# Twenty feed-forward tiles as seven block products instead of eight, with activations and residual parked in memory

## The chip, the core and the metric

The kernel runs on one core of one Trainium2 chip. The number that counts is the device time of one execution in microseconds (us), the median of several runs. The profile is one execution taken by the hardware profiler; it records every instruction of the engines: TensorE (PE) for matmuls with its weight loads (PEld), VectorE (DVE), ScalarE (ACT), GpSimd (POOL), and the queue of SyncE (SP) that issues the DMA transfers.

## The reference

One encoder block on 512 tokens of width 2048, in float32. What matters here is its second half, the gated feed-forward (`D_FF` is 5632):

```python
x = x + jnp.concatenate([y_f, y_g], axis=-1) @ w_out[l]
h2 = rmsnorm(x, norm_ffn[l])
x = x + (jax.nn.silu(h2 @ w_gate[l]) * (h2 @ w_up[l])) @ w_down[l]
return rmsnorm(x, norm_final)
```

## The kernel before

Every product of two float32 matrices is done as three matmuls. Each operand is split into `hi`, a rounded copy (ACT writes it), and `lo`, the remainder `raw - hi` (DVE writes it); `hi*hi`, `hi*lo` and `lo*hi` accumulate in one PSUM bank (`mm3`). So a weight tile of 128x1024 costs one ACT copy and one DVE subtraction before TensorE may use it (`split`, `split_weights`). The buffers for `hi` and for `lo` are three deep.

The feed-forward has 44 tiles of 128 features. `GateUp(f, up, kk)` is one unit: half of the depth (8 of 16 slices of 128) of the gate or the up projection of tile `f`, 24 matmuls of 128x512. The second half of a tile's gate is followed by a DVE multiply with the token scales `rg` and a tanh on ACT; the second half of its up by two DVE operations that complete the activation in `act`. Two tiles share one slot of 128x2x512, four tiles make a quad.

The down projection already uses block products. For each of ten quads and each half `np_` of the output columns there are seven instead of eight (`Product`, in the order 1, 2, 5, 6, 3, 7, 4), 12 matmuls of 128x512 each. Before a product runs, DVE forms a sum of activation blocks (`x`) for four of the seven and a sum of weight blocks (`r[..]`) for four of the seven; ACT and DVE split both. After it, DVE adds the two PSUM banks into the residual `x2`, or into `usum`, which `Fold` later adds to three of the four blocks. Product 2 goes on accumulating in the banks of product 1, and product 3 in those of product 5, after DVE has read what stood there. The last two pairs of tiles are multiplied in the usual way (`Split`, `Last`, `Tail`).

The program order is written by hand. `drive` walks through `items`; ahead of each item `k` it emits the preparation of item `k + 2` on ACT and DVE, then the item's matmuls (`run`), then what follows them (`out`), and what follows on the next item's turn (`late`). Each engine works through its own list in this order. In `items` a quad's 14 products stand one by one between the 16 `GateUp` units of the next quad, so a product always has a unit on both sides. Raw weights come through the SP queue, at most three `GateUp` tiles ahead (`load_unit`), and the blocks of `w_down` up to eight items ahead.

The residual `x2` (8 slots of 4 KB per partition) and the activations stay in SBUF throughout. The pool of such slots (`spool`) holds 25.

Of the kernel before, what the change touches and what calls it, by code (L numbers as in the profile page):

```python
# [16 lines left out]
P = 128  # L17
# [16 lines left out]

QUADS = 10


@with_exitstack
def encoder_block(ctx, tc, a, out):
# [129 lines left out]
    def split(src, dst):  # L169
        nc.scalar.copy(dst[0], src)  # L170
        nc.vector.tensor_sub(dst[1], src, dst[0])  # L171
# [49 lines left out]
    def both(x, c):  # L221
        return x[0][:, c], x[1][:, c]
# [210 lines left out]
    def x2c(m, n):  # L433
        return x2[m][n // 2][:, (n % 2) * S : (n % 2 + 1) * S]

    xss = const.tile([P, NT, 4], F32, name="xss")
    h2 = []

    def transposes(n):
        for i in range(4):  # L440
            c = 4 * n + i
            ps = bank(f"xt{c}")
            for m in range(NT):
                nc.tensor.transpose(ps[:, m * P : (m + 1) * P], x2c(m, n)[:, i * P : (i + 1) * P], ident)
# [31 lines left out]


    fss = const.tile([P, NT, 4], F32, name="fss")
    act = [None] * FT

# [23 lines left out]

    pgu = {}
    acts = {}

    class GateUp(RawUnit):
        def __init__(self, f, up, kk):
# [12 lines left out]
        def out(self):  # L522
            if self.kk == 0:
                return
            f = self.f
            if not self.up:
                if f == 0:
                    ffn_scales()
                if f % 2 == 0:
                    acts[f // 2] = slot(f"act{f // 2}", F32, (P, 2, S))  # L530
                self.z = acts[f // 2][:, f % 2, :]
                self.s = small.tile([P, S], F32, tag="act", bufs=1, name=f"s{f}")
                nc.vector.tensor_mul(self.z, pgu[0], rg)
                nc.scalar.activation(self.s, self.z, AF.Tanh, scale=0.5)
                pgu["gate"] = self
            else:
                s, z = pgu["gate"].s, pgu["gate"].z
                nc.vector.scalar_tensor_tensor(s, pgu[1], 0.5, rg, op0=ALU.mult, op1=ALU.mult)
                nc.vector.tensor_mul(z, z, s)

        def late(self):
            if self.kk and not self.up:
                nc.vector.scalar_tensor_tensor(self.z, self.s, 1.0, self.z, op0=ALU.add, op1=ALU.mult)
# [8 lines left out]


    ORDER = (1, 2, 5, 6, 3, 7, 4)
    usum = [slot(f"u{np_}", F32, (P, 2, S)) for np_ in range(2)]
    for np_ in range(2):
        nc.gpsimd.memset(usum[np_], 0.0)

    def out_block(k, t, np_):

        return x2c(2 * (k // 10 - 1) + t, 2 * np_ + k % 10 - 1)

    PRODUCTS = {}

    class Product(Item):
# [89 lines left out]
    def down(i, m, n, w):  # L655
        ps = bank(f"l{i}_{m}_{n}")
        for j in range(2):
            c = slice(j * S, (j + 1) * S)
            mm3(ps, both(rest[2 * i + j], slice(m * P, (m + 1) * P)), (w.hi[:, c], w.lo[:, c]), j == 0, j == 1)
        return ps  # L660

    class Last(RawUnit):
# [9 lines left out]
        def out(self):  # L672
            tails[self.n].prep()
            for m in range(NT):
                nc.vector.tensor_add(x2c(m, self.n), self.ps[m], x2c(m, self.n))

    class Tail(RawUnit):

# [19 lines left out]
                rest.append(p)  # L698


    items = []
    pending = []
    for q in range(FT // 4):
        for i in range(16):
            items.append(GateUp(4 * q + i // 4, i // 2 % 2, i % 2))
            if i > 0 and pending:
                items.append(pending.pop(0))
            if q == QUADS and i in (8, 14):
                items.append(Split(0) if i == 8 else Fold(0))
        pending = [Product(q, np_, i) for np_ in range(2) for i in ORDER]  # L710
    items += [Fold(1), Split(1)]
    items += [Last(n) for n in range(4)]

    tails = [Tail(n) for n in range(4)]
    units = [x for x in items if isinstance(x, RawUnit)]
    units[-1:] = [tails[0], units[-1], *tails[1:]]

    def load_unit():
        if units:
            units.pop(0).load()  # L720

    def drive(items, lead=8):

        for _ in range(3):
            load_unit()
        works = [x for x in items if not isinstance(x, (Split, Fold))]
        loaded = set()
        for x in works[:2]:
            yield x
            load_unit()  # L730
        behind = []
        k = 0
        for x in items:
            if x in works:
                if k + 2 < len(works):
                    y = works[k + 2]
                    y.prep()
                    if isinstance(y, RawUnit):
                        load_unit()
                for y in works[k : k + lead]:  # L740
                    if isinstance(y, Product) and y not in loaded:
                        y.load()
                        loaded.add(y)
                k += 1
            for y in behind:
                y.late()
            x.run()
            x.out()
            behind = [x]

    ENG = mybir.EngineType
    with tc.manual_schedule(engines={ENG.SP, ENG.PE, ENG.DVE, ENG.Activation, ENG.Pool}):
        for x in drive(items):
            x.prep()


    gB = [slot(f"gB{i}") for i in range(2)]
# [95 lines left out]
```

## Time and profile before

| | |
|---|---|
| runs | 1886.45 us median of 3 (1886.31 to 1886.63) |
| profiled execution | 1886.81 us, span of the instructions 1885.0 us |
| TensorE busy | 1864.7 us, 8370 matmuls |
| VectorE busy | 1210.0 us, 1541 instructions |
| ScalarE busy | 657.0 us, 844 instructions |
| moved by DMA | 197.52 MB, mean 105 GB/s |
| granted TensorE clock | 0.997 of full speed |

The profiled execution is 0.36 us above the median of the runs. The feed-forward begins at 486.3 us of the span and runs to its end. A matmul's row in the profile shows its latency; matmuls overlap, so the pace of TensorE is read from the distance between the starts of two neighbours, or from a count in a stretch that is fully busy.

### The profile page before, as it was taken

The page shows a single profiled execution, that of the slowest core. Times are in us where ns is not written, and L with a number is a line of the kernel's source. Part 1 is how long each engine was busy: PE and PEld are TensorE (multiplying, and loading weights), DVE is VectorE, ACT ScalarE, POOL GpSimd, SP SyncE. Part 2 cuts the span into 40 slices and gives each one's busy share as a digit, 9 for nine tenths or more (in the row PEclk, how much of TensorE's full clock was granted, in tenths as well). Part 3 has the DMA queues.
Part 4 walks back from the last instruction along what each step waited for, and adds up shares of the span by engine and source line. Part 5 has one row for each costly group of instructions (what it writes and reads, how often), then busy time and mean ns, then how long its engine had stood idle before and what let it go on. Part 6 is the DMA issues. An engine that isn't in the chain of part 4 may idle for free.

```text
span 1885.0 us, 20877 instructions
## 1 busy us (share of the span) xinstructions
PE 1864.7 (99%) x8370; PEld 1546.7 (82%) x8370; DVE 1210.0 (64%) x1541; ACT 657.0 (35%) x844; POOL 68.6 (4%) x54
## 2 busy tenths in 40 slices
PE   9999999999999999999999999999999999999996
PEld 7888788888888888888888888888888888888885
DVE  7455654333435767767767677677676776776787
ACT  6335633232323333333333333333332332332334
POOL 5001101000000000000000000000000000000004
PEclk9999999999999999999999999999999999999998
DMA  6222224422232232233133222332333223222323
GB/s 246 91 79 101 90 72 141 145 90 90 91 121 90 101 112 91 91 121 112 67 112 112 101 100 90 112 112 72 107 112 111 90 90 118 106 86 97 108 89 124
DMA packets 55969, 197.52 MB, mean 105 GB/s; under 512 B 6592, under 2 KB 6720, under 8 KB 55872
## 3 DMA queue, kind: packets, MB, share of 16 engines
q1 hardware_dynamic: 55584, 195.15, 29.7%
q8 instruction: 65, 1.06, 0.2%
q0 software_dynamic: 288, 1.05, 0.2%
q14 instruction: 32, 0.26, 0.0%
HBM read 191.98 MB, written 4.19 MB: 104 GB/s over the span
## 4 chain that ended last, share of the span: by engine, by line
PE 97%; DVE 1%; ACT 1%; DMA 0%; issue 0%; SPq 0%; POOL 0%; ACTq 0%; DVEq 0%
PE up L82 8%; PE g L82 8%; PE up L83 8%; PE g L83 8%; PE g L84 8%; PE up L84 8%; PE d L625 7%; PE d L624 7%; PE d L623 7%; PE o L84 3%; PE o L82 3%; PE o L83 3%; PE v L82 2%; PE v L84 2%; PE v L83 2%; PE a L84 1%
## 5 line engine op out<-in xcount | busy, mean ns | idle before, releaser
L82 PE MATMUL up<-h2hi,hi_up 128*128 128x512 f32 x704 | 274.0, 389 | 0.0
L82 PE MATMUL g<-h2hi,hi_g 128*128 128x512 f32 x704 | 274.0, 389 | 0.0
L84 PE MATMUL g<-h2hi,lo_g 128*128 128x512 f32 x704 | 273.9, 389 | 0.0
L84 PE MATMUL up<-h2hi,lo_up 128*128 128x512 f32 x704 | 273.9, 389 | 0.0
L83 PE MATMUL up<-h2lo,hi_up 128*128 128x512 f32 x704 | 273.9, 389 | 0.0
L83 PE MATMUL g<-h2lo,hi_g 128*128 128x512 f32 x704 | 273.9, 389 | 0.0
L171 DVE TENSOR_TENSOR lo_d<-w,hi_d 128x1024 fp32r<-128x1024 f32 x140 | 171.5, 1225 | 82.9 <-ACT hi_d L170 82.9
L623 PE MATMUL d<-hi_d,X 128*128 128x512 f32 x560 | 217.8, 389 | 0.0
L624 PE MATMUL d<-lo_d,X 128*128 128x512 f32 x560 | 217.8, 389 | 0.0
L625 PE MATMUL d<-hi_d,X 128*128 128x512 f32 x560 | 217.8, 389 | 0.0
L170 ACT CAST hi_d<-w 128x1024 fp32r<-128x1024 f32 x140 | 147.2, 1051 | 184.9 <-issue 40.0
L84 PEld LDWEIGHTS up<-h2hi,lo_up 128*128 128x128 f32 x704 | 132.1, 188 | 27.5
L84 PEld LDWEIGHTS g<-h2hi,lo_g 128*128 128x128 f32 x704 | 132.1, 188 | 27.5
L82 PEld LDWEIGHTS up<-h2hi,hi_up 128*128 128x128 f32 x704 | 132.1, 188 | 27.4
L82 PEld LDWEIGHTS g<-h2hi,hi_g 128*128 128x128 f32 x704 | 132.1, 188 | 27.4
L83 PEld LDWEIGHTS g<-h2lo,hi_g 128*128 128x128 f32 x704 | 132.1, 188 | 27.4
L83 PEld LDWEIGHTS up<-h2lo,hi_up 128*128 128x128 f32 x704 | 132.1, 188 | 27.4
L170 ACT CAST X<-x 128x512 fp32r<-128x512 f32 x80 | 49.8, 622 | 270.4 <-DVE x L587 102.7
L171 DVE TENSOR_TENSOR lo_up<-raw_up,hi_up 128x1024 fp32r<-128x1024 f32 x88 | 107.3, 1220 | 47.6 <-ACT hi_up L170 47.6
L170 ACT CAST hi_g<-raw_g 128x1024 fp32r<-128x1024 f32 x88 | 92.5, 1052 | 112.7 <-PE d L625 56.5
L634 DVE TENSOR_TENSOR x<-d,x 128x512 f32<-128x512 f32 x200 | 130.8, 684 | 0.0
L170 ACT CAST hi_up<-raw_up 128x1024 fp32r<-128x1024 f32 x88 | 92.5, 1052 | 104.9 <-PE g L83 57.7
(254 smaller groups left out, 2930.7 us busy)
## 6 DMA issues: line engine op xcount, KB each, us to landing
raw_g<-in_w_gate SPq DMA_DIRECT2D x88, 512.0 KB, 3.3
raw_up<-in_w_up SPq DMA_DIRECT2D x88, 512.0 KB, 3.3
w<-in_w_down SPq DMA_DIRECT2D x80, 512.0 KB, 4.5
raw_o<-in_w_out SPq DMA_DIRECT2D x32, 512.0 KB, 3.2
raw_v<-in_w_v SPq DMA_DIRECT2D x16, 512.0 KB, 3.2
raw_u<-in_w_u SPq DMA_DIRECT2D x16, 512.0 KB, 3.3
raw_a<-in_w_a SPq DMA_DIRECT2D x15, 512.0 KB, 3.8
x<-in_x SPq DMA_DIRECT2D x8, 512.0 KB, 8.2
```

The costliest lines, as they stand in the source:

```text
L82: mm(ps, lhs[0], rhs[0], start=first, stop=False)
L83: mm(ps, lhs[0], rhs[1], start=False, stop=False)
L84: mm(ps, lhs[1], rhs[0], start=False, stop=last)
L170: nc.scalar.copy(dst[0], src)
L171: nc.vector.tensor_sub(dst[1], src, dst[0])
L623: mm(p, X[:, 0, j, l], hi, start=j == 0 and not more, stop=False, skip_group_check=True)
L624: mm(p, X[:, 0, j, l], lo, start=False, stop=False, skip_group_check=True)
L625: mm(p, X[:, 1, j, l], hi, start=False, stop=j == 1, skip_group_check=True)
L634: nc.vector.tensor_add(d, self.ps[t], d)
```

## The change

The gate and the up projection of tiles 4 to 23 become block products too. A pair of tiles (256 features), 2048 deep, times 512 tokens is cut in two along each of the three sides: 8 products of 128 features x 1024 deep x 256 tokens, of which 7 are done (`Block`, in the order 1, 6, 2, 7, 5, 4, 3). A block is 24 matmuls of 128x256. One `Matrix` is the gate or the up of one pair; there are 20.

- The sums of token blocks (`Forms`, 8 of them) are made once, while the first four tiles run as before. Their split copies and raw sums lie in 16 of the 26 slots until the last block has run.
- The sums of weight blocks are made by DVE for every matrix: two adds ahead of block 6, one ahead of block 7 (its result is used by block 4), one subtraction ahead of block 5.
- After a block DVE (after blocks 1 and 2 ACT) takes 128x256 out of PSUM. After block 3 come the scales and the tanh, now on 128x1024.
- No product of the down projection stands among the blocks. All 140 stand among the 80 units of tiles 24 to 43: of the 76 gaps between units that get any, 64 get two products and 12 get one.
- To make room, the residual goes to DRAM (`xd`, 8 stores) before the feed-forward and comes back in 16 loads of 256 KB when tile 24 has begun (`Outputs`); activations of the ten quads go to DRAM as they are made (`ad`, 20 stores of 512 KB, from the POOL queue) and come back two at a time with the first product of a quad (20 loads).
- `Fold(0)` moves from between the last units to the end, beside `Fold(1)`.

The names: `lo_gb7_6` is the remainder of the weights for block 6 of the gate of pair 7 (`gb`), `upb` is the up; `o_gb7` collects the gate, `t_` holds partial sums, `th` the tanh; `d3_0_1` is product 1 of quad 3, column half 0, `X` its activation operand, `ac` a reloaded activation pair.

First place: VectorE, where the gate of a pair ends and the up begins. Before, the gate of tile 14 ended like this (a product of quad 2 in between):

```order
L171 TENSOR_TENSOR lo_up14_0_6390<-raw_up14_0_6221,hi_up14_0_6389 128x1024
L533 TENSOR_TENSOR act7_6419<-g14_6341,rstdB_99 128x512
L585 TENSOR_TENSOR x2_1_5_6423<-act4_5097,act5_5553 128x512
L596 TENSOR_TENSOR w11_2_1_6164<-w11_2_1_6164,w12_2_1_6282 128x1024
L171 TENSOR_TENSOR X2_1_5_6425<-x2_1_5_6423,X2_1_5_6425 128x512
L171 TENSOR_TENSOR lo_d2_1_5_6430<-w11_2_1_6164,hi_d2_1_5_6429 128x1024
L543 SCALAR_TENSOR_TENSOR act7_6419<-s14_6420,act7_6419 128x512
```

Now the gate of tiles 14 and 15 ends like this:

```order
L633 TENSOR_TENSOR w12_upb7_6512<-w12_upb7_6512,w22_upb7_6514 128x1024
L634 TENSOR_TENSOR w11_upb7_6510<-w11_upb7_6510,w12_upb7_6512 128x1024
L174 TENSOR_TENSOR lo_upb7_6_6732<-w11_upb7_6510,hi_upb7_6_6731 128x1024
L671 TENSOR_TENSOR o_gb7_6550<-gb7_5_6673,t_gb7_6551 128x256
L676 TENSOR_TENSOR o_gb7_6550<-o_gb7_6550,rstdB_101 128x1024
L174 TENSOR_TENSOR lo_upb7_2_6770<-w21_upb7_6548,hi_upb7_2_6769 128x1024
L687 SCALAR_TENSOR_TENSOR o_gb7_6550<-th7_6766,o_gb7_6550 128x1024
L636 TENSOR_TENSOR w21_upb7_6548<-w21_upb7_6548,w11_upb7_6510 128x1024
L174 TENSOR_TENSOR lo_upb7_7_6806<-w12_upb7_6512,hi_upb7_7_6805 128x1024
L661 TENSOR_TENSOR t_upb7_6777<-upb7_6_6809,t_upb7_6777 128x256
L638 TENSOR_TENSOR w11_upb7_6510<-w11_upb7_6510,w22_upb7_6514 128x1024
L174 TENSOR_TENSOR lo_upb7_5_6837<-w11_upb7_6510,hi_upb7_5_6836 128x1024
```

The work that ends the gate (L671, L676, L687) now stands between the sums and remainders of the weights for the up's blocks 6, 2, 7 and 5, each of which TensorE takes up within a block or two.

Second place: VectorE, where products 1 and 2 of quad 3 are prepared. Before, a unit's remainder and its activation stand between them:

```order
L171 TENSOR_TENSOR X3_0_1_6765<-act6_5963,X3_0_1_6765 128x512
L171 TENSOR_TENSOR lo_d3_0_1_6769<-w11_3_0_6620,hi_d3_0_1_6768 128x1024
L171 TENSOR_TENSOR lo_up16_0_6798<-raw_up16_0_6680,hi_up16_0_6797 128x1024
L533 TENSOR_TENSOR act8_6829<-g16_6772,rstdB_99 128x512
L171 TENSOR_TENSOR X3_0_2_6833<-act7_6419,X3_0_2_6833 128x512
L171 TENSOR_TENSOR lo_d3_0_2_6837<-w21_3_0_6682,hi_d3_0_2_6836 128x1024
L543 SCALAR_TENSOR_TENSOR act8_6829<-s16_6830,act8_6829 128x512
L634 TENSOR_TENSOR u0_3607<-d3_0_1_0_6841,u0_3607 128x512
L634 TENSOR_TENSOR u0_3607<-d3_0_1_1_6842,u0_3607 128x512
```

Now the two products are neighbours:

```order
L174 TENSOR_TENSOR X3_0_1_10717<-ac6_10550,X3_0_1_10717 128x512
L174 TENSOR_TENSOR lo_d3_0_1_10721<-w11_3_0_10554,hi_d3_0_1_10720 128x1024
L782 TENSOR_TENSOR x21_1_8859<-d2_1_4_0_10724,x21_1_8859 128x512
L782 TENSOR_TENSOR x21_1_8859<-d2_1_4_1_10725,x21_1_8859 128x512
L174 TENSOR_TENSOR X3_0_2_10740<-ac7_10552,X3_0_2_10740 128x512
L174 TENSOR_TENSOR lo_d3_0_2_10744<-w21_3_0_10580,hi_d3_0_2_10743 128x1024
L174 TENSOR_TENSOR lo_up30_1_10775<-raw_up30_1_10611,hi_up30_1_10774 128x1024
L782 TENSOR_TENSOR u0_8834<-d3_0_1_0_10778,u0_8834 128x512
L782 TENSOR_TENSOR u0_8834<-d3_0_1_1_10779,u0_8834 128x512
```

Product 2 follows product 1 on TensorE with no unit in between, and the two adds that must read product 1 out of its banks stand behind the remainders of product 2 and of the next unit.

The diff, cut to what the prediction speaks of:

```diff
+FIRST, BLOCKS = 4, 20
...
-    spool = ctx.enter_context(tc.tile_pool(name="s", bufs=25))
+    spool = ctx.enter_context(tc.tile_pool(name="s", bufs=26))
...
+        if n % 2:
+            for m in range(NT):
+                nc.gpsimd.dma_start(xd[m, n // 2], x2[m][n // 2])
...
+    class Forms(Item):
+        def out(self):
+            j = self.j
+            raw = slot(f"hr{j}", F32, (P, 2, S))
+            x = slot(f"hx{j}", F32, (P, 4, H))
+            for i, h in enumerate((h2[j], h2[KT // 2 + j])):
+                nc.vector.tensor_add(raw[:, i, :], h[0], h[1])
...
+            for i, (fa, fb) in enumerate(((5, 6), (3, 7))):
+                t = slot(f"hf{j}_{i}", F32R, (P, 2, 2, H))
+                split(x[:, 2 * i : 2 * i + 2, :], (t[:, 0], t[:, 1]))
...
+    GORDER = (1, 6, 2, 7, 5, 4, 3)
...
+    class Block(Item):
...
+        def prep(self):
+            i, r = self.i, self.m.r
+            add, sub = nc.vector.tensor_add, nc.vector.tensor_sub
+            if i == 6:
+                add(r[12], r[12], r[22])
+                add(r[11], r[11], r[12])
+            elif i == 7:
+                add(r[21], r[21], r[11])
+            elif i == 5:
+                sub(r[11], r[11], r[22])
+            self.split_weights(r[{1: 11, 6: 11, 2: 21, 7: 12, 5: 11, 4: 21, 3: 22}[i]], f"{self.m.name}_{i}")
...
+            ps = m.r["ps", i][:, :H]
+            for j in range(KT // 2):
+                c = slice(j * P, (j + 1) * P)
+                mm3b(ps, (self.hi[:, c], self.lo[:, c]), forms[i, j], j == 0 and not more, j == KT // 2 - 1)
...
+            else:
+                nc.vector.tensor_sub(o[:, 1, :H], ps, u)
+                scale = rg.unsqueeze(1).to_broadcast([P, 2, S])
+                if not m.up:
+                    pgu["o"] = o
+                    pgu["t"] = slot(f"th{m.p}", F32, (P, 2, S))
+                    nc.vector.tensor_mul(o, o, scale)
+                    nc.scalar.activation(pgu["t"], o, AF.Tanh, scale=0.5)
+                else:
+                    nc.vector.scalar_tensor_tensor(o, o, 0.5, scale, op0=ALU.mult, op1=ALU.mult)
+                    nc.vector.tensor_mul(pgu["o"], pgu["o"], o)
+                    acts[m.p] = pgu["o"]
+                    keep(m.p)
...
+            if self.i == 1 and self.np_ == 0:
+                for p in (2 * self.q, 2 * self.q + 1):
+                    acts[p] = slot(f"ac{p}", F32, (P, 2, S))
+                    nc.sync.dma_start(acts[p], ad[p])
...
+    for p in range(FIRST // 2, (FIRST + BLOCKS) // 2):
+        for up in range(2):
+            m = Matrix(p, up)
+            items += [Block(m, i) for i in GORDER]
...
+        want = min(len(products), len(products) * max(0, n + 1 - LAG) // (len(units) - LAG - 1))
+        items += products[done:want]
...
+    items += [Fold(0), Fold(1), Split(1)]
```

More of the change, by code (lines that the diff above doesn't have):

```diff
@@ L434, in x2c @@
         return x2[m][n // 2][:, (n % 2) * S : (n % 2 + 1) * S]
+    xd = dram.tile([NT, 2, P, U], F32, name="xd")
     xss = const.tile([P, NT, 4], F32, name="xss")
@@ L478, in encoder_block @@
     fss = const.tile([P, NT, 4], F32, name="fss")
-    act = [None] * FT
+    ad = dram.tile([FT // 2, P, 2, S], F32, name="ad")
+    cs_ = {}
     class Item:
@@ L506, in encoder_block, with keep @@
     acts = {}
+    def keep(p):
+        if p < FT // 2 - 2:
+            nc.gpsimd.dma_start(ad[p], acts.pop(p))
     class GateUp(RawUnit):
@@ L539, in out @@
                 nc.vector.tensor_mul(z, z, s)
+                if f % 2:
+                    keep(f // 2)
         def late(self):
@@ L554, in encoder_block, with xc, __init__ @@
     ORDER = (1, 2, 5, 6, 3, 7, 4)
-    usum = [slot(f"u{np_}", F32, (P, 2, S)) for np_ in range(2)]
-    for np_ in range(2):
-        nc.gpsimd.memset(usum[np_], 0.0)
+    usum = [None, None]
     def out_block(k, t, np_):
-        return x2c(2 * (k // 10 - 1) + t, 2 * np_ + k % 10 - 1)
+        return cs_[k, np_][:, t, :]
+    def xc(m, n):
+        return cs_[10 * (m // 2 + 1) + n % 2 + 1, n // 2][:, m % 2, :]
+    forms = {}
+    class Forms(Item):
+        def __init__(self, j):
+            self.j = j
+        def out(self):
[4 more added lines that the diff above has]
+                nc.vector.tensor_add(raw[:, i, :], h[0], h[1])
+            A11, A21, A12, A22 = raw[:, 0, :H], raw[:, 0, H:], raw[:, 1, :H], raw[:, 1, H:]
+            nc.vector.tensor_sub(x[:, 0, :], A21, A22)
+            nc.vector.tensor_sub(x[:, 1, :], x[:, 0, :], A11)
+            nc.vector.tensor_add(x[:, 2, :], x[:, 1, :], A12)
+            nc.vector.tensor_sub(x[:, 3, :], A11, A21)
+            for i, (fa, fb) in enumerate(((5, 6), (3, 7))):
+                t = slot(f"hf{j}_{i}", F32R, (P, 2, 2, H))
+                split(x[:, 2 * i : 2 * i + 2, :], (t[:, 0], t[:, 1]))
+                forms[fa, j], forms[fb, j] = ((t[:, 0, k, :], t[:, 1, k, :]) for k in range(2))
+            for i, (k, c) in {1: (j, 0), 2: (KT // 2 + j, 0), 4: (KT // 2 + j, H)}.items():
+                forms[i, j] = both(h2[k], slice(c, c + H))
@@ new lines, in mm3b, with out @@
+    def mm3b(ps, lhs, rhs, first, last):
+        mm(ps, lhs[0], rhs[0], start=first, stop=False, skip_group_check=True)
+        mm(ps, lhs[0], rhs[1], start=False, stop=False, skip_group_check=True)
+        mm(ps, lhs[1], rhs[0], start=False, stop=last, skip_group_check=True)
+    class Outputs(Item):
+        def out(self):
+            for np_ in range(2):
+                usum[np_] = slot(f"u{np_}", F32, (P, 2, S))
+                nc.gpsimd.memset(usum[np_], 0.0)
+                for k in (11, 22, 12, 21):
+                    t = cs_[k, np_] = slot(f"x{k}_{np_}", F32, (P, 2, S))
+                    n = 2 * np_ + k % 10 - 1
+                    for i in range(2):
+                        nc.sync.dma_start(t[:, i, :], xd[2 * (k // 10 - 1) + i, np_, :, (n % 2) * S : (n % 2 + 1) * S])
@@ L701, in encoder_block @@
     items = []
[L702 to L711, printed above, removed]
+    units = [(f, up, kk) for f in range(FT) for up in range(2) for kk in range(2)]
@@ new lines, in encoder_block @@
+    for n, x in enumerate(units[: 4 * FIRST]):
+        items.append(GateUp(*x))
+        if n % 2 and n // 2 < KT // 2:
+            items.append(Forms(n // 2))
+    for p in range(FIRST // 2, (FIRST + BLOCKS) // 2):
+        for up in range(2):
+            m = Matrix(p, up)
+            items += [Block(m, i) for i in GORDER]
+    units = units[4 * (FIRST + BLOCKS) :]
+    products = [Product(q, np_, i) for q in range(QUADS) for np_ in range(2) for i in ORDER]
+    done = 0
+    LAG = 3
+    for n, x in enumerate(units):
+        items.append(GateUp(*x))
+        if n == 0:
+            items.append(Outputs())
+        if n == len(units) - 8:
+            items.append(Split(0))
+        want = min(len(products), len(products) * max(0, n + 1 - LAG) // (len(units) - LAG - 1))
+        items += products[done:want]
+        done = want
@@ L712, in encoder_block @@
+    items += [Fold(0), Fold(1), Split(1)]
     items += [Last(n) for n in range(4)]
     tails = [Tail(n) for n in range(4)]
-    units = [x for x in items if isinstance(x, RawUnit)]
-    units[-1:] = [tails[0], units[-1], *tails[1:]]
-    def load_unit():
[L719 to L727, printed above, removed]
+    works = [x for x in items if not isinstance(x, (Split, Fold, Forms, Outputs))]
@@ new lines, in encoder_block, with load_ahead @@
+    todo = [x for x in works if isinstance(x, RawUnit)]
+    todo[-1:] = [tails[0], todo[-1], *tails[1:]]
+    ahead = [0]
+    loaded = set()
+    def load_unit():
+        ahead[0] -= 1
+    def load_ahead(k, lead=6):
+        for y in works[k : k + lead]:
+            if isinstance(y, RawUnit):
+                while todo and ahead[0] < 3 and y not in loaded:
+                    x = todo.pop(0)
+                    x.load()
+                    loaded.add(x)
+                    ahead[0] += 1
+            elif y not in loaded:
+                y.load()
+                loaded.add(y)
+        if k + lead > len(works):
+            while todo and ahead[0] < 3:
+                todo.pop(0).load()
+                ahead[0] += 1
@@ L728, in drive @@
+    def drive():
+        load_ahead(0)
         for x in works[:2]:
-            yield x
-            load_unit()
+            x.prep()
+            if isinstance(x, RawUnit):
+                load_unit()
+        load_ahead(2)
         behind = []
@@ L739, in drive @@
                         load_unit()
[L740 to L743, printed above, removed]
+                load_ahead(k + 3)
                 k += 1
```

58 lines of the change are left out of this document (49 added, 9 removed).

## The prediction

> **What bounds the kernel now.** I read the page's busy times first, then the chain of work that ended last, then stretches of the feed-forward, then single instructions.
>
> ```profile
> PE 1864.7 (99%) x8370; PEld 1546.7 (82%) x8370; DVE 1210.0 (64%) x1541; ACT 657.0 (35%) x844; POOL 68.6 (4%) x54
> PE 97%; DVE 1%; ACT 1%; DMA 0%; issue 0%; SPq 0%; POOL 0%; ACTq 0%; DVEq 0%
> ...
> 500.00:600.00 100.00, 100.00 (x443) 82.79 (x442) 41.32 (x47) 25.27 (x28) 0.00 (x0) 1.00 0.31 106
> 1000.00:1400.00 400.00, 400.00 (x1766) 331.20 (x1766) 282.51 (x346) 131.16 (x152) 0.00 (x0) 1.00 0.30 103
> ```
>
> TensorE is the bound, and in the feed-forward it never pauses: 400 us hold 1766 matmuls of 128x512, one each 0.2265 us. But the second row shows what the 64% of the whole hides: while units and products alternate, VectorE is busy 71% of the time. In the first 100 us, where there are only units, it is busy 41%. A change that takes time from TensorE and gives work to VectorE has to be followed on both.
>
> **TensorE's part of the change.** The kernel has matmuls of 128x256 in its Fourier part, back to back:
>
> ```profile
> 105.26 0.28 PE L82 MATMUL dft<-tabs_hi,cls 128*128 128x256 f32 x1
> 105.37 0.28 PE L83 MATMUL dft<-tabs_lo,cls 128*128 128x256 f32 x1
> ...
> 105.85 0.28 PE L84 MATMUL dft<-tabs_hi,cls 128*128 128x256 f32 x1
> 105.97 0.22 PE L82 MATMUL dft<-tabs_hi,cls 128*128 128x128 f32 x1
> ```
>
> Six take 105.97 - 105.26 = 0.71 us, 0.1183 each: not half of 0.2265 but 52%. A pair of tiles, gate and up, was 192 x 0.2265 = 43.5 us and becomes 2 x 7 x 24 = 336 x 0.1183 = 39.75. Ten pairs save **37.6 us**, if TensorE never waits. A block lasts 2.84 us, against 5.44 for a unit.
>
> **VectorE's prices.**
>
> ```profile
> 1001.36 1.22 DVE L602 TENSOR_TENSOR w<-w,w 128x1024 f32<-128x1024 f32 x1
> 1002.50 0.69 DVE L171 TENSOR_TENSOR X<-act,X 128x512 fp32r<-128x512 f32 x1
> 1002.69 1.05 ACT L170 CAST hi_d<-w 128x1024 fp32r<-128x1024 f32 x1 [3.97 <-DVE w L602]
> 1003.77 1.23 DVE L171 TENSOR_TENSOR lo_d<-w,hi_d 128x1024 fp32r<-128x1024 f32 x1 [0.59 <-ACT hi_d L170]
> 1004.87 1.05 ACT L170 CAST hi_g<-raw_g 128x1024 fp32r<-128x1024 f32 x1 [1.13 <-PE d L625]
> 1005.52 0.68 DVE L637 TENSOR_TENSOR x<-x,d 128x512 f32<-128x512 f32 x1
> 1005.83 0.62 ACT L170 CAST X<-act 128x512 fp32r<-128x512 f32 x1
> 1006.11 0.68 DVE L634 TENSOR_TENSOR x<-d,x 128x512 f32<-128x512 f32 x1
> ...
> 1009.34 0.39 PE L83 MATMUL up<-h2lo,hi_up 128*128 128x512 f32 x1
> 1009.56 0.39 PE L84 MATMUL up<-h2hi,lo_up 128*128 128x512 f32 x1
> 1009.79 0.39 PE L623 MATMUL d<-hi_d,X 128*128 128x512 f32 x1
> 1009.81 1.05 ACT L170 CAST hi_d<-w 128x1024 fp32r<-128x1024 f32 x1 [3.36 <-issue]
> 1009.99 0.69 DVE L538 SCALAR_TENSOR_TENSOR s<-up,rstdB 128x512 f32<-128x512 f32 x1 [1.46 <-PE up L84]
> 1010.72 0.69 DVE L539 TENSOR_TENSOR act<-act,s 128x512 f32<-128x512 f32 x1
> ```
>
> Start to start, a 1024-wide DVE operation holds the engine 1.14 us (1001.36 to 1002.50), a 512-wide one 0.6 (1005.52 to 1006.11). One that reads its predecessor's result waits for its end: 0.73 instead of 0.6 (1009.99 to 1010.72). For 128x256 no row fits; the line through both widths gives 0.33, result after 0.42. An ACT copy of 1024 takes 1.05, its successor starts after 0.96 (1004.87 to 1005.83). ACT starts 0.11 after a DVE result (1002.69), DVE 0.03 after ACT's (1003.77). DVE reads a bank 0.20 after TensorE has gone on (1009.99 against 1009.79); ACT may refill a `hi` buffer 0.47 after the start of its last reader (1009.81 against 1009.34), 0.36 for the shorter matmuls.
>
> That chained operations pay more speaks against the Trainium skill, "VectorE: DVE Perf Modes", section "The DRAIN you can't avoid", which finds that a semaphore after each operation costs nothing extra. By that page the two hand-overs below would lose 0.7 us less per pair, 7 us in all, and the sum would be 1927; the row decides.
>
> **The stretch of blocks.** VectorE's own work per pair is 22 operations of 1024 on weights and 4 on activations, 26 x 1.135 = 29.5, ten of 256, 3.3, some 0.8 for chained ones: 33.6 us under 39.75. Throughput is no bound; the order may be. In the list printed for the first place, let 0 be the start of the up's block 1. The two sums for block 6 start at -2.31 and -1.05 and end at 0.17; ACT's `hi` runs 0.28 to 1.33; `lo` for block 6 starts at 1.37. The gate's last subtraction follows at 2.51, its scaling at 2.97, done 4.19. Now ACT is asked for the tanh (4.29 to 5.34) ahead of block 2's `hi` (5.25 to 6.30); `lo` starts at 6.34, done 7.56. Blocks 1 and 6 are over at 5.68; block 2 needs `lo` from its third matmul on, 0.24 later, so it starts at 7.38: **1.70 lost**. Behind it DVE does the late operation (7.48), the sum (8.61) and `lo` (9.75) for block 7, which starts at 10.78 instead of 10.22, 0.57 lost; then the subtraction for block 5 (11.21), ACT 12.54 to 13.59, `lo` until 14.85: 1.05 lost. Blocks 4, 3 and the next 1 and 6 follow without a pause. Where an up ends, two 1024-wide operations stand instead of scaling and tanh; the same steps give 0.72 at block 2 and 0.48 at block 5. Together 4.52 a pair, so 44.27 against 43.5 before: the stretch costs **+7.6 us** where TensorE alone would save 37.6. The bounds are -37.6 (all of it overlaps) and, if the next `lo` after each of the four ACT copies that wait for a sum had to wait in full (1.19 each) on top, +55.
>
> **The stretch of units and products.** DVE's work per product, from these rows:
>
> ```profile
> L171 DVE TENSOR_TENSOR lo_d<-w,hi_d 128x1024 fp32r<-128x1024 f32 x140 | 171.5, 1225 | 82.9 <-ACT hi_d L170 82.9
> L634 DVE TENSOR_TENSOR x<-d,x 128x512 f32<-128x512 f32 x200 | 130.8, 684 | 0.0
> L171 DVE TENSOR_TENSOR lo_up<-raw_up,hi_up 128x1024 fp32r<-128x1024 f32 x88 | 107.3, 1220 | 47.6 <-ACT hi_up L170 47.6
> L171 DVE TENSOR_TENSOR lo_g<-raw_g,hi_g 128x1024 fp32r<-128x1024 f32 x87 | 106.1, 1220 | 28.5 <-ACT hi_g L170 28.5
> L171 DVE TENSOR_TENSOR X<-x,X 128x512 fp32r<-128x512 f32 x80 | 55.0, 688 | 13.8 <-ACT X L170 13.8
> L634 DVE TENSOR_TENSOR u<-d,u 128x512 f32<-128x512 f32 x80 | 52.1, 685 | 0.0
> L171 DVE TENSOR_TENSOR X<-act,X 128x512 fp32r<-128x512 f32 x60 | 41.3, 688 | 12.8 <-ACT X L170 12.1
> L533 DVE TENSOR_TENSOR act<-g,rstdB 128x512 f32<-128x512 f32 x44 | 30.4, 692 | 126.5 <-PE g L84 126.4
> ```
>
> One `lo` of 1024 and one of 512, 2.3 adds and subtractions into the residual or `u` (200 + 80 + 40 over 140) and, for four in seven, a sum of each width: 1.13 + 0.6 + 1.37 + 0.65 + 0.34 = 4.09 us, against 12 x 0.2265 = 2.72 on TensorE. A unit is the reverse: 1.76 against 5.44. Unit and product in turn need 5.85 of 8.16; unit and two products need 9.94 of 10.87. Waits for ACT come on top: 82.9 / 140 = 0.59 a product at its `lo`. With these alone 11.12, and with those for `X` (26.6 / 140 = 0.19) and for the units' `lo` (76.1 / 175 = 0.43) as in the rows, 11.94. So 64 such cycles lose between 0 (all waits covered) and 64 x 1.07 = 68 us. Within them stands a wait that is new: product 2 adds to the banks of product 1. In the list printed for the second place, with 0 at the start of product 1, DVE is at `X` and `lo` of product 2 at 0.82 and 1.42, at the unit's `lo` at 2.55 and only at 3.69 at the first add, though product 1 ended at 2.72; product 2 starts at 4.42, 1.70 late. The same steps through the ten quads find some 10 us at second products and 24 at other products whose `lo` is late. I take **+34**, the middle of the bounds. Laid over the old order these steps leave TensorE without a pause and let DVE wait 132 us at L533, where the row has 126.5.
>
> **What else moves.** `Forms`: 8 x 4 us on DVE in the first 87 us, 41% busy: hidden. Two `Fold`s at the end put 3.6 us more in front of the last tiles' adds, which free the banks that `Last(2)` needs: **+2** (0 to 4). Stores and reloads add 28 MB at some 100 GB/s of traffic, ahead of need. The one tight place is the return of the residual:
>
> ```profile
> GB/s 246 91 79 101 90 72 141 145 90 90 91 121 90 101 112 91 91 121 112 67 112 112 101 100 90 112 112 72 107 112 111 90 90 118 106 86 97 108 89 124
> x<-in_x SPq DMA_DIRECT2D x8, 512.0 KB, 8.2
> ```
>
> 4.2 MB at the page's fastest 246 GB/s are 17 us, and the weights of product 6 and of unit 25 queue behind them on SP; the fourth product's sum wants them some 34 us after tile 24 begins. Price 0 to 8; I take **+4**, since the queue also waits there for the last gate's store to free a raw buffer.
>
> **Sum.** 1886.8 (profiled) + 7.6 + 34 + 2 + 4 = 1934.4; the median lies 0.4 below its profiled run: **1934 us**.
>
> **Rivals.**
> *Engines keep ahead (faster).* VectorE's own work is less than TensorE's in both stretches (33.6 of 39.75, 9.94 of 10.87); if ACT runs ahead, nothing is lost: 1886.5 - 37.6 + 2 = 1851. It decides once all pauses stay under 37.6 us. Against it: a `hi` buffer is free only when the third block before is done, so ACT cannot run ahead. 8%; another 3% that it comes out even.
> *Only the products' stretch is covered.* 1886.5 + 7.6 + 2 + 4 = 1900. For it: DVE's waits for units in the rows (126.5) shrink first. 17%.
> *The products' stretch at its bound,* 68: 1968. For it: my steps make DVE wait a little longer than the row, so it has slightly more to do than I price. 14%.
> *Each 128x256 matmul waits for its weights.* The page's weight loads take 1546.7 / 8370 = 0.185 us; if they set the pace, 20 x 168 x 0.185 = 622 us replace 435, and the time is 2073 or more. The Fourier rows at 0.118 speak against it: 3%. The Trainium skill, "TensorE: Matmul & The Clock Gate", part 3, "The mechanism", has weight loads overlap running matmuls only in other row groups; these use all rows, and neither stretch of the trace agrees.
>
> **How the numbers follow.** Forecast (1912 to 1955) 55%, the others as above. The range 1893 to 1972 leaves out the fast cases, the weight loads and the end of the third rival, 17 in 100. By 0.2%, about 4 us, which a measurement of this kernel can tell: faster 8%, same 3%, slower 89%.
>
> **What would show it.** In the blocks, matmuls start 0.118 apart, with pauses ahead of blocks 2, 5 and 7 that end on DVE's `lo`; VectorE is busy over 80% there and over 90% among the products; TensorE's busy share falls to 95% or less; the chain shows DVE and ACT. Wrong I would be if TensorE shows no pauses (then 1851), or if they end on a DMA.

## The result and the profile after

The changed kernel takes **1936.9 us** (median of 4 runs, 1935.7 to 1938.9), the kernel before 1886.4 in the same session: **1.0269 times** the time, 95% interval 1.0251 to 1.0287, so 50.5 us slower. The forecast was 1934, with a range of 1893 to 1972. Saved matmul time was there, and a good deal more was lost in pauses of TensorE.

The page of the changed kernel, its busy times and its chain of work that ended last:

```profile
PE 1863.0 (96%) x9810; PEld 1592.1 (82%) x9810; DVE 1433.8 (74%) x1805; ACT 729.4 (38%) x950; POOL 84.3 (4%) x82
...
PE 66%; DVE 22%; ACT 6%; issue 5%; DMA 0%; ACTq 0%; POOL 0%; SPq 0%; DVEq 0%
```

TensorE's share fell from 99% to 96%, which looks harmless. The chain says more: TensorE carried 97% of it, now 66%, and VectorE and ACT have 28% between them. DMA has none.

Three stretches of the changed kernel; the columns are length, then busy time and count on TensorE, its weight loads, VectorE, ACT and POOL, then the granted clock, DMA share and GB/s. The first has only units (with `Forms`), the second only blocks, the third units and products:

```profile
500.00:560.00 60.00, 60.00 (x267) 49.69 (x266) 45.16 (x70) 20.15 (x26) 0.53 (x1) 1.00 0.42 149
600.00:1000.00 400.00, 374.60 (x3010) 363.62 (x3009) 309.67 (x324) 144.14 (x171) 4.79 (x9) 1.00 0.33 105
1100.00:1800.00 700.00, 683.66 (x2968) 555.42 (x2967) 611.25 (x775) 262.76 (x319) 3.72 (x7) 1.00 0.33 118
```

VectorE is busy 75, 77 and 87% of the time; where units and products alternated before, it was 71%. In the first stretch `Forms` raised it from 41 to 75% and TensorE still has not one gap.

What TensorE waited for in the changed kernel (total us, times, longest):

```profile
PE upb L692 <- DVE lo_upb L174: 15.1, 30, 0.8
PE d L772 <- DVE lo_d L174: 8.4, 14, 1.1
PE d L771 <- DVE u L782: 8.0, 8, 2.2
PE gb L692 <- DVE lo_gb L174: 6.9, 19, 0.5
PE upb L690 <- ACT t_upb L659: 5.8, 10, 0.6
PE d L771 <- ACT hi_d L173: 3.1, 6, 0.8
PE l L85 <- DVE x L823: 2.0, 1, 2.0
```

These are idle times after the recorded end of a matmul. Matmuls overlap, so a pause counted from start to start is mostly some 0.16 us longer than its row. All the new waits end on VectorE or ACT, none on a transfer.

The end of a gate and the start of an up in the changed kernel, the first place of the order above (start, duration, then idle time before it and what ended that):

```profile
684.44 1.22 DVE L633 TENSOR_TENSOR w_upb<-w_upb,w_upb 128x1024 f32<-128x1024 f32 x1
685.69 1.22 DVE L634 TENSOR_TENSOR w_upb<-w_upb,w_upb 128x1024 f32<-128x1024 f32 x1
687.02 1.05 ACT L173 CAST hi_upb<-w_upb 128x1024 fp32r<-128x1024 f32 x1 [4.88 <-PE gb L692]
688.10 1.23 DVE L174 TENSOR_TENSOR lo_upb<-w_upb,hi_upb 128x1024 fp32r<-128x1024 f32 x1 [1.19 <-ACT hi_upb L173]
689.24 0.42 DVE L671 TENSOR_TENSOR o_gb<-gb,t_gb 128x256 f32<-128x256 f32 x1
689.69 1.22 DVE L676 TENSOR_TENSOR o_gb<-o_gb,rstdB 128x1024 f32<-128x1024 f32 x1
690.95 1.06 ACT L677 ACTIVATE th<-o_gb 128x1024 f32<-128x1024 f32 x1 [2.88 <-DVE o_gb L676]
691.91 1.03 ACT L173 CAST hi_upb<-w_upb 128x1024 fp32r<-128x1024 f32 x1
692.85 0.36 ACT L659 COPY t_upb<-upb 128x256 f32<-128x256 f32 x1
692.98 1.22 DVE L174 TENSOR_TENSOR lo_upb<-w_upb,hi_upb 128x1024 fp32r<-128x1024 f32 x1 [2.06 <-ACT hi_upb L173]
...
693.27 0.38 PE L690 MATMUL upb<-h2hi,hi_upb 128*128 128x256 f32 x1 [0.57 <-ACT t_upb L659]
...
694.12 1.22 DVE L687 SCALAR_TENSOR_TENSOR o_gb<-th,o_gb 128x1024 f32<-128x1024 f32 x1
...
694.26 0.38 PE L692 MATMUL upb<-h2hi,lo_upb 128*128 128x256 f32 x1 [0.49 <-DVE lo_upb L174]
```

Read it as a relay: sums (684.44, 685.69), ACT's `hi`, VectorE's `lo`, scaling (689.69), tanh (690.95), and only then ACT's `hi` for block 2 and VectorE's `lo`. The engine that TensorE waits for has itself just waited 2.06 us.

The pace of TensorE where nothing pauses, first and last of 117 matmuls in a row:

```profile
612.50 0.28 PE L690 MATMUL upb<-hf,hi_upb 128*128 128x256 f32 x1
...
626.41 0.28 PE L692 MATMUL gb<-hf,lo_gb 128*128 128x256 f32 x1
```

13.91 us over 116 steps are 0.1199 each.

### The profile page after: what moved, and what is told of

Its sections match the earlier page's. It is cut to its first block, busy times and chain, and to the rows that moved or that the text cites. A ratio compares the mean times of both kernels' runs of the same rounds, so it can differ in the third digit from the quotient of the medians.

```text
span 1933.9 us, 24401 instructions
## 1 busy us (share of the span) xinstructions
PE 1863.0 (96%) x9810; PEld 1592.1 (82%) x9810; DVE 1433.8 (74%) x1805; ACT 729.4 (38%) x950; POOL 84.3 (4%) x82
## 4 chain that ended last, share of the span: by engine, by line
PE 66%; DVE 22%; ACT 6%; issue 5%; DMA 0%; ACTq 0%; POOL 0%; SPq 0%; DVEq 0%
PE d L772 4%; PE d L773 4%; PE d L771 4%; PE g L85 3%; PE g L86 3%; PE g L87 3%; PE up L87 3%; PE up L85 3%; PE up L86 3%; PE o L87 3%; PE o L85 3%; PE o L86 3%; DVE lo_d L174 3%; DVE lo_upb L174 2%; DVE lo_gb L174 2%
## 5 line engine op out<-in xcount | busy, mean ns | idle before, releaser
L87 PE MATMUL up<-h2hi,lo_up 128*128 128x512 f32 x384 | 149.8, 390 | 0.6 <-DVE lo_up L174 0.6
L85 PE MATMUL up<-h2hi,hi_up 128*128 128x512 f32 x384 | 149.5, 389 | 0.0
L85 PE MATMUL g<-h2hi,hi_g 128*128 128x512 f32 x384 | 149.5, 389 | 0.0
L86 PE MATMUL up<-h2lo,hi_up 128*128 128x512 f32 x384 | 149.4, 389 | 0.0
L86 PE MATMUL g<-h2lo,hi_g 128*128 128x512 f32 x384 | 149.4, 389 | 0.0
L87 PE MATMUL g<-h2hi,lo_g 128*128 128x512 f32 x384 | 149.4, 389 | 0.0
L772 PEld LDWEIGHTS d<-lo_d,X 128*128 128x128 f32 x560 | 105.5, 188 | 39.3 <-DVE lo_d L174 18.0
L771 PEld LDWEIGHTS d<-hi_d,X 128*128 128x128 f32 x560 | 105.5, 188 | 38.7 <-issue 11.2
L782 DVE TENSOR_TENSOR x<-d,x 128x512 f32<-128x512 f32 x200 | 129.8, 681 | 0.0
L773 PEld LDWEIGHTS d<-hi_d,X 128*128 128x128 f32 x560 | 105.5, 188 | 21.3
L174 DVE TENSOR_TENSOR lo_upb<-w_upb,hi_upb 128x1024 fp32r<-128x1024 f32 x70 | 85.5, 1223 | 49.8 <-ACT hi_upb L173 49.8
L692 PE MATMUL upb<-hf,lo_upb 128*128 128x256 f32 x320 | 92.5, 289 | 10.2 <-DVE lo_upb L174 10.2
```

The costliest lines, as they stand in the source:

```text
L85: mm(ps, lhs[0], rhs[0], start=first, stop=False)
L86: mm(ps, lhs[0], rhs[1], start=False, stop=False)
L87: mm(ps, lhs[1], rhs[0], start=False, stop=last)
L692: mm(ps, lhs[1], rhs[0], start=False, stop=last, skip_group_check=True)
L771: mm(p, X[:, 0, j, l], hi, start=j == 0 and not more, stop=False, skip_group_check=True)
L772: mm(p, X[:, 0, j, l], lo, start=False, stop=False, skip_group_check=True)
```

## The experiments

All times are medians; each ratio is against the kernel before in the same session (1885.9 for the first four, 1886.4 for the others).

### The blocks as plain units, the rest as changed

```diff
...
-            items += [Block(m, i) for i in GORDER]
+    items += [GateUp(*x) for x in units[4 * FIRST : 4 * (FIRST + BLOCKS)]]
```

The loop around the blocks and the `Forms` go with them.

> Tiles 4 to 23 are computed as ordinary units again, in their stretch of their own; the token sums (Forms) are gone; residual and activations still go through memory and all 140 products still stand among the units of tiles 24 to 43. Theory A (the order of VectorE's list pauses TensorE, in both stretches separately): the stretch of tiles 4 to 23 takes 435 us instead of the 450 of the changed kernel, the last stretch keeps its 34 us of pauses: 1936.9 - 15 = 1922 us. Rival B (the way through memory makes data late) says the same here, since that way is kept. Rival C (the block products upset what follows, for example by the slots or raw buffers they hold at the boundary): most of the loss goes with them, 1890 us or less.

1923.5 us, ratio 1.0199 (1.0184 to 1.0214). Theory A; Rival B says the same time and is left to the next run. Without one block the kernel is still 37.6 us slower than before; the blocks themselves cost the remaining 13.4. TensorE's waits in this run:

```profile
PE d L772 <- DVE lo_d L174: 8.8, 14, 1.1
PE d L771 <- DVE u L782: 8.1, 8, 2.2
PE d L771 <- ACT hi_d L173: 3.4, 6, 0.8
PE l L85 <- DVE x L823: 2.0, 1, 2.0
```

Row by row they are nearly the products' waits of the changed kernel (8.4, 8.0, 3.1 and 2.0): the loss among the products does not depend on the blocks.

### The memory way alone

No blocks; products one at a time between units again.

```diff
-FIRST, BLOCKS = 4, 20
+FIRST, BLOCKS = 4, 0
...
-        want = min(len(products), len(products) * max(0, n + 1 - LAG) // (len(units) - LAG - 1))
+        q, i = divmod(max(n - 4, 0), 16)
+        want = 14 * min(q, 9) + min(14, i) if n < 148 else 126 + min(14, 14 * (n - 147) // 11)
...
-    def load_ahead(k, lead=6):
+    def load_ahead(k, lead=3):
```

The last line lets weights be loaded fewer items ahead than in the changed kernel.

> No block products at all: all 44 tiles are ordinary units, the products stand one by one between them as before the change (the last quad's 14 between 11 units), but residual and activations go through memory as in the changed kernel, and the Folds stand at the end. Weight loads run up to five items ahead instead of eight. Theory A: the way through memory is hidden, 1886.4 + 2.4 for the Folds and 0 to 3 for the crowded last quad: 1889 to 1892 us. Rival B: a good part of the 34 us of the last stretch comes back, 1905 to 1925 us.

1888.6 us, ratio 1.0015 (1.0006 to 1.0024). Theory A, 0.4 us below its range; Rival B is out. Of the 2.7 us, 2.0 are the wait at L823 behind the two folds. Stores, reloads and the residual's return are hidden at this pace of products; that they are hidden at two products to a unit too, only the trace of the changed kernel says, in which no wait of TensorE ends on a transfer.

### The products' weight sums on GpSimd

```diff
-                nc.vector.tensor_add(r[11], r[11], r[12])
+                nc.gpsimd.tensor_add(r[11], r[11], r[12])
```

and the same for the other three of each seven.

> The changed kernel, with the four weight sums of every seven down products (80 operations of 128x1024) on GpSimd instead of VectorE; transfers and TensorE's list stay. Theory A: VectorE's list in the last stretch is 91 us shorter; if GpSimd takes 2.0 to 3.0 us for one (its 128x512 rows take 1.3), the pauses of 34 us shrink to 10 to 20: 1913 to 1923 us. Rival B: unchanged, 1935 to 1939.

1960.3 us, ratio 1.039 (1.0373 to 1.0407): **both theories missed**, by 21 us at least. Around one sum in this run:

```profile
1299.97 1.22 DVE L174 TENSOR_TENSOR lo_d<-w,hi_d 128x1024 fp32r<-128x1024 f32 x1
1301.11 1.28 DVE L782 TENSOR_TENSOR x<-d,x 128x512 f32<-128x512 f32 x2
1301.27 2.40 POOL L744 TENSOR_TENSOR w<-w,w 128x1024 f32<-128x1024 f32 x1 [20.41 <-DVE lo_d L174]
1302.31 1.92 DVE L174 TENSOR_TENSOR X<-ac,X 128x512 fp32r<-128x512 f32 x1
1304.15 1.21 DVE L174 TENSOR_TENSOR lo_d<-w,hi_d 128x1024 fp32r<-128x1024 f32 x1
```

The sum takes 2.40 us on GpSimd, against 1.22 on VectorE, and while it runs VectorE's 512-wide operation takes 1.92 instead of 0.69: it ends 0.56 after the sum. The two adds of L782 ahead of it, which read one operand from PSUM, are not stretched (1.28 for two). The groups of this run say the same (busy, mean ns, idle before):

```profile
L782 DVE TENSOR_TENSOR x<-d,x 128x512 f32<-128x512 f32 x200 | 130.0, 681 | 0.1
L174 DVE TENSOR_TENSOR X<-x,X 128x512 fp32r<-128x512 f32 x80 | 81.5, 1019 | 55.0 <-ACT X L173 55.0
...
L735 DVE TENSOR_TENSOR x<-x,ac 128x512 f32<-128x512 f32 x20 | 32.9, 1644 | 0.0
```

In the changed kernel the last two have 685 and 680 ns. VectorE was rid of 80 sums and waited for them in other places. A part of the loss is the clock of TensorE, which falls to half for spells of 3.41 us after pauses (last section): in the feed-forward of this run's trace the granted clock is 0.5 for ten such windows, in that of the changed kernel for two. The matmuls in them lose some 15 us here and some 3 there, so about 12 of the 27 us between the two profiled spans (1961.0 and 1933.9). How the rest divides between the longer sum on the path and the stretched operations was not separated.

### Scaling and tanh one item later

The gate's scaling and tanh, and the up's last two operations, move from `out` of block 3 to `late`, behind the preparation of block 2. The operation that uses the tanh moves back as well, to `late` of the up's block 1.

```diff
-                    nc.vector.tensor_mul(o, o, scale)
-                    nc.scalar.activation(pgu["t"], o, AF.Tanh, scale=0.5)
...
+        def late(self):
+            if self.i == 3:
+                if not m.up:
+                    nc.vector.tensor_mul(o, o, scale)
+                    nc.scalar.activation(pgu["t"], o, AF.Tanh, scale=0.5)
...
```

> The changed kernel, with the scaling and tanh at the end of a gate, and the two last operations of an up, emitted one item later, behind the preparation of the next matrix's block 2 instead of ahead of it; the work is the same. Theory A (at the hand-over it is the order that counts, the lo of block 2 stands behind work that nobody waits for): the pause of 1.7 us at block 2 shrinks, a pair takes 43.6 instead of 44.6 us, 1936.9 - 10 = 1927 us. Rival D (VectorE and ScalarE are simply full in this stretch): the same amount of work, no gain, 1935 to 1939.

1926.7 us, ratio 1.0216 (1.02 to 1.0231). Theory A: 10.2 us of the blocks' loss come from the place of these instructions, and TensorE's waits for `lo_upb` fall from 15.1 us in 30 to 7.6 in 10. The products' waits stay as they were.

### No weight sums in the products

```diff
-            if i == 5:
-                nc.vector.tensor_add(r[11], r[11], r[12])
-            elif i == 6:
...
```

> The changed kernel without the four 1024-wide VectorE sums of weights in each seven products, in all ten groups of four tiles (80 operations; the products then multiply the unsummed weights, so the output is not the reference's); weights, loads, order, blocks and everything else as in the changed kernel. It asks whether VectorE's work per product is what the +34.5 us of the stretch of units and products consist of. Theory A (VectorE is late with lo because of its own work): a product needs 4.09 - 0.65 = 3.44 us of VectorE, so a unit and two products need 1.76 + 6.88 = 8.64, with the waits for ACT (0.59 and 0.19 a product, 0.43 a unit) 10.6 of 10.87 us: nothing is late any more but the second products that wait for a bank, 7 to 8 us. 1936.9 - 34.5 + 7.5 = 1910 us (1904 to 1917), no wait of TensorE for lo_d worth more than 2 us. Theory B (the loss comes from the turn of products and units itself: bank waits, ACT's copies, hi buffers; the sums lie in VectorE's gaps): 1930 to 1937. Theory C (the waits move to ACT, which then has a sum less to wait for but no free hi buffer): 1918 to 1929, with TensorE's waits on hi_d over 10 us.

1914.1 us, ratio 1.0146 (1.0132 to 1.016). Theory A; the waits of TensorE that are left among the products are those for a bank:

```profile
PE d L763 <- DVE u L774: 6.5, 8, 2.2
```

Not one wait for `lo_d` or `hi_d` remains. With 0.65 us less VectorE work a product, 22.8 us are back: two thirds of the loss among the products go with VectorE's sums. A sum also stands ahead of ACT's `hi` and VectorE's `lo` of the same product, so the run does not tell the sheer amount of work from the sum's place in that chain.

### Eight tiles as blocks

```diff
-FIRST, BLOCKS = 4, 20
+FIRST, BLOCKS = 4, 8
```

> The changed kernel with 8 tiles (4 to 11) as blocks instead of 20; tiles 12 to 43 are plain units, so the 140 products stand among 128 units instead of 80. Memory way, forms, folds as in the changed kernel. Theory A (two separate losses: 1.1 us per pair of blocks against units and some 4 us once for the first pair, and crowding of products, which at 1.1 products to a unit is over, since unit and product in turn need 5.85 of 8.16 us of VectorE): 1886.4 + 4 x 1.1 + 4 + 2.4 for the folds = 1897 us, some 3 us more if four second products still meet the bank of the first: 1895 to 1903. Theory B (the +34.5 us belong to the products wherever they stand, a quarter of a microsecond each, for their activations through memory or the new order of loads): 1886.4 + 8.4 + 2.4 + 34.5 = 1932, 1925 to 1937. Theory C (the loss in the blocks is one of the whole stretch and not per pair): 1886.4 + 15.3 + 2.4 = 1904, up to 1908.

1904.4 us, ratio 1.0092 (1.0077 to 1.0108). B is out. The number is 1.4 above A's range and at C's; the trace decides for A. Four pairs of blocks take 182.4 us (574.3 to 756.7) against 174.0 of units, 8.4 more, which is A's 4 x 1.1 + 4; C asked for 15.3. And 140 products among 128 units lose 7.3 us (1083.6 against 1076.3): four waits for a bank, 4.0 us from start to start, and something that no theory had, matmuls at half speed behind such a wait (last section), which cost 1.6 us here and 1.6 more behind the folds. Less these two, the time lies in A's range:

```profile
1105.22 0.47 PE L771 MATMUL d<-hi_d,X 128*128 128x512 f32 x1 [2.23 <-DVE u L782]
...
1106.78 0.63 PE L771 MATMUL d<-hi_d,X 128*128 128x512 f32 x1
...
1109.34 0.63 PE L85 MATMUL up<-h2hi,hi_up 128*128 128x512 f32 x1
...
1110.10 0.39 PE L87 MATMUL up<-h2hi,lo_up 128*128 128x512 f32 x1
```

### Another order of the products

```diff
-    ORDER = (1, 2, 5, 6, 3, 7, 4)
+    ORDER = (1, 5, 2, 6, 3, 7, 4)
```

(and the banks kept for each of products 1 and 5).

> The changed kernel with each seven products in the order 1, 5, 2, 6, 3, 7, 4 instead of 1, 2, 5, 6, 3, 7, 4, so that product 2, which adds to the banks of product 1, never stands right behind it; nothing else. It asks whether the new wait for those banks (8.0 us in the trace of the changed kernel, eight times) is a loss of its own. Theory A (it is, but VectorE, which is late anyway, keeps a part: the sum for product 5 is wanted earlier): stepped through the ten groups by the rows of the prediction, 6 us of it are won: 1931 us, 1928 to 1934, TensorE's waits of d on u under 2 us and those on lo_d grown by 1 to 3. Theory B (VectorE's total work in the stretch sets its length, and where it is waited for does not matter): 1936 to 1938, with the 8 us now under lo_d. Theory C (won in full): 1928 or less, with lo_d not grown.

1930.5 us, ratio 1.023 (1.0216 to 1.0244). Theory A: the wait for the bank is gone, and a part of it stands under `lo_d`, 10.4 us now against 8.4:

```profile
PE d L771 <- DVE lo_d L174: 10.4, 18, 1.1
```

### Units among the blocks

```diff
-FIRST, BLOCKS = 4, 20
+FIRST, BLOCKS = 4, 12
...
-            items += [Block(m, i) for i in GORDER]
+            for k, i in enumerate(GORDER):
+                if k in (1,):
+                    items.append(GateUp(*next(others)))
+                items.append(Block(m, i))
...
```

together with the order 1, 5, 2, 6, 3, 7, 4 and `o_gb` in a slot.

> A version meant to beat both: 12 tiles (4 to 15) as blocks; in each gate and each up matrix one plain unit (of tiles 16 to 18, 12 units in all) stands between block 1 and block 6, that is where VectorE and ACT are late after the end of the matrix before; the 140 products stand among 100 units in the order 1, 5, 2, 6, 3, 7, 4; the gate's result lies in a buffer of the common pool instead of a raw buffer. Everything is computed. A unit lasts 5.44 us on TensorE and asks 1.76 of VectorE, so 3.7 us of slack stand against the 2.8 us that a gate's blocks, and 1.7 that an up's blocks lose. Theory A (the slack takes up every pause): 6 pairs of tiles at 336 x 0.120 = 40.3 instead of 43.5 us save 19 us; folds +2.4, the first pair +4, at 1.4 products to a unit almost no loss among the products: 1886.4 - 19 + 6.4 = 1874 us, 1869 to 1881. Theory B (the pauses stay, because a unit's hi waits for the same three buffers and its lo joins the same queue): 1886.4 + 6 x 1.1 + 6.4 = 1899, 1893 to 1905. Theory C (pauses gone, but crowding at 1.4 products to a unit, half way between the 1.1 without and the 1.75 with 34.5 us of loss, costs 16 us): 1890, 1883 to 1893.

**1872.9 us, ratio 0.9928 (0.9916 to 0.994)**: 13.5 us faster than the kernel before, and Theory A's 1874. Busy times and chain of this run, then its stretch of blocks and its stretch of products:

```profile
PE 1848.5 (99%) x9234; PEld 1573.7 (84%) x9234; DVE 1359.6 (73%) x1725; ACT 705.7 (38%) x914; POOL 83.9 (4%) x82
...
PE 96%; DVE 2%; ACT 1%; issue 0%; DMA 0%; POOL 0%; SPq 0%; ACTq 0%; DVEq 0%
```

```profile
600.00:860.00 260.00, 260.00 (x1954) 250.41 (x1953) 196.39 (x204) 94.86 (x109) 3.20 (x6) 1.00 0.33 111
1000.00:1800.00 800.00, 800.00 (x3531) 662.40 (x3531) 673.98 (x845) 297.84 (x357) 4.79 (x9) 1.00 0.32 117
```

TensorE has no gap in either, with VectorE at 76 and 84%. The sum: 2016 matmuls at 0.120 instead of 1152 at 0.2265 save 19.0; the wait behind the folds costs 2.0, the half-speed spell that follows it (last section) 1.6, and two waits at the first pair 1.8. That is -13.6. Fewer block tiles, the unit and the order came together here, so their shares in this run are not told apart.

## Why the prediction was right

**The saving of TensorE** was put at 37.6 us (its own factors give 37.4) and is 32.0: 3360 matmuls at 0.1199 take 402.9 us, not 3360 x 0.1183 = 397.5, against 434.9 for the units. Six Fourier matmuls were too few to read a pace to 1%; that row stands for 5.4 us.

**The stretch of blocks** was priced at +7.6 and takes 450.2 us (572.6 to 1022.8) against 434.9 for the units, **+15.3**. The pauses per pair, 4.52 by the steps, are 4.32: a pair recurs every 44.64 us, of which 40.32 are matmuls. An up loses 3.1 of them and a gate 1.2, against 3.32 and 1.20 by the steps. So on the whole the steps of the relay were right, and the scaling experiment, which moves the scaling, the tanh and the end of an up, and gains 10.2 us, shows that their place is a cause. Two terms were mis-sized: the pace, above, and the first pair, which the text gave nothing. It takes 48.1 us, 3.5 more than the next, since the last `Forms` work stands among its blocks: 0.89 + 0.36 + 0.82 us of waits, and matmuls at half speed behind them. One wait of the relay was overlooked: block 2 also waits for ACT's copy `t_`, queued behind tanh and `hi` (692.85), 5.8 us in all. In the lines above it ends ahead of the wait for `lo` (693.27 against 694.26), so there it does not lengthen the pause.

**The stretch of units and products** was the largest term, +34, "the middle of the bounds", and takes 850.0 us against 3600 x 0.2265 = 815.4, **+34.6**. Its two parts were 10 at second products and 24 at other products that are late. Summed from start to start, the gaps that end on the read of a bank are 9.3 us; those that end on `lo_d` and `hi_d` by name are 15.5. Of the rest, some 5 are gaps at products too short to show as idle time, 1.6 a spell at half speed and 1.1 waits of units for `lo_up`; the remaining 2.4 are spread over the stretch. The experiment without sums gives 23 back; that without neighbours, 6 of the 9.3.

**The folds** were +2 and are +2.3 (the last 192 matmuls take 45.8 us against 43.5).

**The way through memory** was +4 and is nothing. SP issues the 16 reloads in 10.75 us; the last, issued at 1043.1, takes at most 6.8 us to land, so all are there by 1049.9, about 17 us after the first issue, as the prediction had it. The first sum into a reloaded block is at 1054.98, and the room between was enough:

```profile
1032.67 10.75 SPq L705 DMA_DIRECT2D x<-xd  x16
DMA to landing us min/median/max: 4.6/5.6/6.8
1054.98 1.37 DVE L782 TENSOR_TENSOR x<-d,x 128x512 f32<-128x512 f32 x2
```

No product waits for a transfer, and the memory-only run is 2.7 us slower in all, folds included.

The terms add up to 15.3 + 34.6 + 2.3 = 52.2; the profiled span grew by 48.9. 2.0 us of the difference lie ahead of the feed-forward, whose first matmul starts at 484.1 and not 486.1 in this execution, and 0.4 behind the last matmul. The rest is the rounding of the pace: before, the 5856 matmuls of units and products take 1327.5 us, 0.2267 each, which makes 1.0 us on the 5520 that are compared here.

That the forecast of 1934 lies only 3 us beside 1936.9 is in part luck: the blocks were priced 7.7 us too low and the memory 4 too high, and the +34 was taken between bounds of 0 and 68, though close to what the steps had found.

**The signs.** Matmuls 0.12 apart, pauses ahead of blocks 2, 5 and 7 that end on `lo`, VectorE and ACT in the chain: as said. VectorE is busy 77% in the blocks and 87% among the products, not over 80 and 90, and TensorE's share is 96%, not 95: the same pauses that slow TensorE leave VectorE idle too, in the relay.

**The rivals.** "Engines keep ahead" failed for the reason given: by their totals VectorE had room, 33.6 of 39.75 us, and still every third block waited (49 waits for `lo_upb` and `lo_gb` in 140 blocks). "Only the products' stretch is covered" fails on the trace, which shows 34.6 us there, and on the first experiment, which keeps that loss without any block. The price of chained operations: 684.44 to 685.69 is 1.25 for a 1024-wide sum that reads its predecessor's result, 692.98 to 694.12 is 1.14 for an operation that does not. So the row of before, by which the prediction decided against that sentence of the Trainium skill ("VectorE: DVE Perf Modes"), holds here too. Weight loads don't set the pace either: 0.1199, not 0.185.

## What to carry to other kernels

Here seven products instead of eight paid only where the engine that makes the sums had slack next to each product, not on average: twenty tiles in a stretch of their own lost 50 us, and twelve, with a plain unit where the relay of VectorE and ACT was late and fewer products to a unit behind them, won 13. When a schedule is rearranged, write the other engine's work beside each item in a row, and step through the hand-over at the joints. And a wait of TensorE has to be priced with what follows it, below.

## What the runs showed of the hardware

**Half speed after pauses.** In the changed kernel, behind two waits that are 1.3 us apart:

```profile
1774.31 0.50 PE L771 MATMUL d<-hi_d,X 128*128 128x512 f32 x1 [0.82 <-ACT hi_d L173]
1775.57 0.50 PE L772 MATMUL d<-lo_d,X 128*128 128x512 f32 x1 [0.76 <-DVE lo_d L174]
1775.90 0.59 PE L773 MATMUL d<-hi_d,X 128*128 128x512 f32 x1
...
1778.85 0.62 PE L771 MATMUL d<-hi_d,X 128*128 128x512 f32 x1
...
1779.54 0.40 PE L773 MATMUL d<-hi_d,X 128*128 128x512 f32 x1
```

Eight matmuls stand 0.42 apart instead of 0.2265, for 3.4 us; a spell costs 1.6 us. The granted clock says the same. Three stretches of 3.41 us around the lines above (columns as before, the clock third from the end):

```profile
1772.51:1775.92 3.41, 1.83 (x8) 0.97 (x7) 2.83 (x4) 2.63 (x4) 0.00 (x0) 1.00 0.51 154
1775.92:1779.33 3.41, 3.41 (x10) 2.67 (x9) 3.41 (x5) 0.24 (x1) 0.00 (x0) 0.50 0.44 137
1779.33:1782.74 3.41, 3.41 (x16) 2.80 (x15) 2.82 (x5) 2.28 (x3) 0.00 (x0) 1.00 0.04 17
```

The changed kernel has one spell here and one at its first pair, the run with eight tiles three, the fastest kernel one, behind the wait for the folds; the kernel before has none in its feed-forward. Equal waits don't always bring one: the bank waits of 2.2 us at 1504 and 1547 in the changed kernel did not. The traces show what decides. The clock changes on a fixed grid: the two spells of the changed kernel begin at 581.26 and 1775.92, 1194.66 us apart, which is 350 times 3.413. Cut the feed-forwards of all ten traces along this grid, and add up in each window at full clock by how much the starts of matmuls fall behind the paces of 0.2265 and 0.1199: all 22 windows that lose 2.01 us or more (up to 2.85) are followed by one at half clock, and none that loses 2.00 or less is. The window ahead of the spell shown loses 2.13 us; that of the wait at 1547 loses 1.96, with the rest of the wait in the next window. The Trainium skill, "TensorE: Matmul & The Clock Gate", Part 1, has the array at half its clock after an idle window of about 3.4 us, with windows that run freely, and 426.7 ns between cold matmuls of this width. Pace, length and grid agree. But none of these spells followed 3.4 us of idleness: 0.8 twice, or 2.0 to 2.2 once, was enough, if it fell into one window.

**GpSimd beside VectorE.** The stretched operations of the third experiment (0.69 to 1.92 us) read both operands from SBUF; those with one in PSUM kept their time. The Trainium skill, "SBUF — State Buffer", section "Who interferes with whom", says that a VectorE instruction with two SBUF inputs contends with a GpSimd instruction that reads SBUF, and that the later one blocks. The trace agrees: the operation ended 0.56 us after the sum, a little less than its own 0.69, and so did the others (all 17 of L735 that started during a sum ended 0.55 to 0.56 after one). The expectation for that run had left this out.
